# Where the recurrent gates' split input is computed: GpSimd and VectorE behind the scan, or VectorE alone ahead of it

## The chip, the cores and the metric

One core of a Trainium2 chip runs one layer of a hybrid decoder (1024 prompt rows and 8 x 4 sample rows). The metric is the device time of one execution in microseconds; the median of several runs counts.

## The reference, cut to what matters

One layer: an input projection of 1024 to 4864 columns, sliding-window attention, a gated linear recurrence (RG-LRU) with a short convolution ahead of it, gated mixing, an MLP of 4096 and a small embedding gate. All inputs are float32. The part that the change touches:

```python
def rglru(x, h0, wa, ba, wx, bx, lam):
    xb = x.reshape(B, T, RNN_BLOCKS, RNN_BS)
    r = sigmoid(einsum('btnd,nde->btne', xb, wa) + ba)
    i = sigmoid(einsum('btnd,nde->btne', xb, wx) + bx)
    log_a = -RG_C * softplus(-lam) * r
    a = exp(log_a)
    bterm = sqrt(-expm1(2.0 * log_a)) * (i * x)
    bterm = bterm.at[:, 0].add(a[:, 0] * h0)
    h = scan of h_t = a_t * h_{t-1} + bterm_t
...
xc, new_conv = causal_conv(xr, conv_prev, conv_w, conv_b)
h, h_last = rglru(xc, h0, rg_wa, rg_ba, rg_wx, rg_bx, rg_lambda)
rnn = (h * gelu(gr)) @ w_o_rnn
```

## The kernel before, in words

Activations lie transposed: 128 channels on the partitions, T = 1056 columns (1024 prompt, 32 sample) along a row, cut into three chunks of CW = 352. A float32 product is made of three matmuls on rounded parts: an operand is cast to a rounded high part (ScalarE), and its low part, operand minus high part, is a subtraction (VectorE or GpSimd). A chunk of a 1024-row projection is 24 matmuls of 352 columns (lines 228 to 230: high times high, high times low, low weight times high).

Weights arrive one 1024x128 block at a time in `wraw` (two buffers). `weights()` at the head of each `linear` splits the block that comes next, one ahead: ScalarE (or GpSimd) casts `wh` (L152), VectorE subtracts `wl` (L153), and then the next load is issued on SyncE. The recurrence's own weights (`rg`, two 128x128 pairs) are cast by ScalarE (L198) and their low part is taken by GpSimd (L199).

The order of the work is written by hand: each engine does its instructions in the order of the program. `flow` is a list of steps that are due after so many chunks; `flow.step()` after each chunk runs those that are due. A generator handed to `flow.run` goes on at each `yield n` n chunks later.

`recur(j)` runs for j = 0 to 7, one tile of 128 channels each; a tile is
- XR: projection of xr, three chunks, copied out by ScalarE (L807, L809, L810); the convolution is one ScalarE instruction (L817, with L818 for the samples) and six on VectorE (L820, L821), giving `xc`;
- the scan of the tile before, `scan()`: ScalarE's Sqrt (L865), on VectorE the product with `it` (L866), the samples' first terms (L870, L871, L872) and the scan itself (L873); after its `yield` GpSimd writes the states and multiplies with the gelu branch (L875 to L877);
- GR: projection, three chunks, gelu on ScalarE (L887). In it `gates()` runs: after the first chunk it makes `xhl`, the two tiles that hold the high part of one block of 64 channels on 64 partitions and its low part on the other 64 (L832, L833), the low part of block 0 on GpSimd and that of block 1 on VectorE, and lets GpSimd end the scan before; after the second chunk the weights of the next XR are split (L152, L153); after the third the gate matmuls of chunks 0 and 1 run (L847, L848), and their sigmoids (L849, L850) write `rt` and `it`;
- the next tile's XR: behind its first chunk the gate matmuls and sigmoids of chunk 2, then exp, exp, tanh (L855 to L857), GpSimd's `it` times `xc` (L858) and, one chunk later, VectorE's L860.

`rt`, `it`, `a` and `xhl` have one buffer each, so a tile's `rt` is free for the next tile's sigmoids only when the scan, which reads it, has ended. The gate matmuls' results lie in four banks, two per chunk.

Of the kernel before, what the change touches and what calls it, by code (L numbers as in the profile page):

```python
# [14 lines left out]
F32R = mybir.dt.float32r  # L15
AF = mybir.ActivationFunctionType
ALU = mybir.AluOpType

P = 128
# [5 lines left out]
T = NP + NS  # L25
CW = T // 3
# [64 lines left out]
def trunk(ctx: ExitStack, tc: tile.TileContext, I, O):  # L91
    nc = tc.nc
    PE, ACT, DVE, POOL, SP = nc.tensor, nc.scalar, nc.vector, nc.gpsimd, nc.sync

    def f32(ap):
        return ap.bitcast(F32)
# [27 lines left out]
    def bank():  # L124
        return po.tile([P, 512], F32, tag="o", name="o")
# [13 lines left out]
    def divide():  # L139
        if raws:  # L140
            raw, split = raws.popleft()
            ready.append(split(raw))
            fetch()
# [96 lines left out]
    def linear(xk, nk, epilogue):  # L240
        w = weights()
        for c in range(3):
            piece(w, xk, nk, c, epilogue)
            flow.step()
# [82 lines left out]
    def col(name, j, n=1):  # L327
        return vec[:, vec_at[name] + j:vec_at[name] + j + n]
# [65 lines left out]
    def halves(g):  # L394

        return slice(g * HD, (g + 1) * HD), slice((1 - g) * HD, (2 - g) * HD)
# [403 lines left out]
    def recur(j):  # L800
        xr = big.tile([P, T], F32, tag="d6", name="xr")
        xsp = const1.tile([P, NB, 7], F32, tag="xsp", name="xsp", bufs=2)
        POOL.memset(xr[:, 0:3], 0.0)

        def put_xr(c, t0, n, ps):
            if c < 2:
                ACT.copy(xr[:, 3 + t0:3 + t0 + n], ps)  # L807
            else:
                ACT.copy(xr[:, 3 + t0:3 + NP], ps[:, :n - NS])  # L809
                ACT.copy(xsp[:, :, 3:], ps[:, n - NS:].rearrange("p (s t) -> p s t", t=NT))  # L810

        POOL.tensor_copy(xsp[:, :, 0:3], state[:, j, :24].rearrange("p (s w) -> p s w", w=3))
        linear(xnk, KT, put_xr)
        xc = big.tile([P, T], F32, tag="d0", name="xc")
        xcs = xc[:, NP:].rearrange("p (s t) -> p s t", t=NT)
        cw = lambda i: col("cw", i * KT + j)
        ACT.activation(xc[:, :NP], xr[:, 3:3 + NP], AF.Identity, scale=cw(3), bias=col("cb", j))  # L817
        ACT.activation(xcs, xsp[:, :, 3:7], AF.Identity, scale=cw(3), bias=col("cb", j))  # L818
        for i in range(3):
            DVE.scalar_tensor_tensor(xc[:, :NP], xr[:, i:i + NP], cw(i), xc[:, :NP], op0=ALU.mult, op1=ALU.add)  # L820
            DVE.scalar_tensor_tensor(xcs, xsp[:, :, i:i + NT], cw(i), xcs, op0=ALU.mult, op1=ALU.add)  # L821
        POOL.tensor_copy(state[:, j, 32:35], xr[:, NP:NP + 3])
        POOL.tensor_copy(state[:, j, 0:24].rearrange("p (s w) -> p s w", w=3), xsp[:, :, 4:7])
        gl = big.tile([P, T], F32, tag=f"e{j}", name="gl")

        def gates():
            xhl = [big.tile([P, T], F32R, tag=f"d{1 + 2 * b}", name="xhl") for b in range(2)]
            for b, low in enumerate((POOL, DVE)):  # L830
                o, other = halves(b)
                ACT.copy(xhl[b][o], xc[o])  # L832
                low.tensor_tensor(xhl[b][other], xc[o], f32(xhl[b][o]), op=ALU.subtract)  # L833
            for _ in before or ():
                pass
            yield 1
            divide()
            yield 1
            wh, wl = ready.popleft()
            rt = big.tile([P, T], F32, tag="d2", name="rt")  # L840
            it = big.tile([P, T], F32, tag="d4", name="it")
            for c, (t0, n) in enumerate(CH):
                t = slice(t0, t0 + n)
                for b in range(2):
                    o, other = halves(b)
                    ps = bank()[:, :n]
                    PE.matmul(ps, wh[:, b, :], xhl[b][:, t], start=True, stop=False)  # L847
                    PE.matmul(ps, wl[:, b, :], xhl[b][:, t], start=False, stop=True)  # L848
                    ACT.activation(rt[o, t], ps[o], AF.Sigmoid, bias=col("ba", j)[o])  # L849
                    ACT.activation(it[o, t], ps[other], AF.Sigmoid, bias=col("bx", j)[o])  # L850
                if c == 1:
                    yield 1
            a = big.tile([P, T], F32, tag="d7", name="a")
            a2 = big.tile([P, T], F32, tag="d1", name="a2")
            ACT.activation(a2, rt, AF.Exp, scale=nc16[:, j:j + 1])  # L855
            ACT.activation(a, rt, AF.Exp, scale=nc8[:, j:j + 1])
            ACT.activation(rt, rt, AF.Tanh, scale=pc8[:, j:j + 1])  # L857
            POOL.tensor_tensor(it, it, xc, op=ALU.mult)  # L858
            yield 1
            DVE.scalar_tensor_tensor(rt, a2, 1.0, rt, op0=ALU.add, op1=ALU.mult)  # L860
            scans.append((a, rt, it))

        def scan():
            a, th, it = scans.popleft()
            ACT.activation(th, th, AF.Sqrt)  # L865
            DVE.tensor_tensor(th, th, it, op=ALU.mult)  # L866
            a0 = a[:, NP:].rearrange("p (s t) -> p s t", t=NT)[:, :, 0]
            b0 = th[:, NP:].rearrange("p (s t) -> p s t", t=NT)[:, :, 0]
            ah = const1.tile([P, NB], F32, tag="ah", name="ah")
            DVE.tensor_tensor(ah, a0, state[:, j, 24:32], op=ALU.mult)  # L870
            DVE.tensor_tensor(b0, b0, ah, op=ALU.add)  # L871
            DVE.memset(a0, 0.0)  # L872
            DVE.tensor_tensor_scan(a, a, th, 0.0, op0=ALU.mult, op1=ALU.add)  # L873
            yield
            POOL.tensor_copy(state[:, j, 35:36], a[:, NP - 1:NP])  # L875
            POOL.tensor_copy(state[:, j, 24:32], a[:, NP:].rearrange("p (s t) -> p s t", t=NT)[:, :, NT - 1])
            POOL.tensor_tensor(gl, a, gl, op=ALU.mult)  # L877
            rnn.append(gl)

        before = None  # L880
        if j:
            before = scan_of.popleft()()
            next(before)
        scan_of.append(scan)
        flow.run(gates(), 1)
        linear(xnk, KT,
               lambda c, t0, n, ps: ACT.activation(gl[:, t0:t0 + n], ps, AF.Gelu_apprx_tanh))  # L887

    for j in range(KT):
        recur(j)  # L890
# [418 lines left out]
    for j in range(KT):  # L1309
        j2, h2 = ((2, 1), (3, 1), (0, 1), (1, 1))[j % 4]  # L1310
        e = hidden_rows(j2, h2, F32, "e")
        for h in range(2):
            for c in range(2):
                o = slice(HALF[h].start + c * CQ, HALF[h].start + (c + 1) * CQ)
# [164 lines left out]
```

## Time and profile before

| | us |
|---|---|
| runs of the kernel, median of 3 | 1657.32 (1652.21 to 1663.13) |
| the profiled execution, its own time | 1662.28 |
| its span, first to last instruction | 1660.5 |

The profile is of one execution. Times in rows are in us from the start of the span, durations of single instructions in us or, in the grouped view, in ns. In a timeline row stand start, duration, engine, line, operation, output and inputs, shape and count, and in brackets how long the engine had been idle and what released it. PE is TensorE's matmuls, PEld its weight loads, DVE VectorE, ACT ScalarE, POOL GpSimd, SPq SyncE's queue. A duration contains some overlap with the next instruction on the engine.

### The profile page before, as it was taken

Reading aid. Unit: us, or ns where it says so; the run is one execution under the profiler, and the core shown is the slowest. Engines: PE = TensorE matmul, PEld = TensorE weight load, DVE = VectorE, ACT = ScalarE, POOL = GpSimd, SP = SyncE. Lnnn points to the kernel's source line nnn. Section 1 sums busy time; section 2 is a strip of 40 time slices with the busy share of each in tenths; the row PEclk is TensorE's granted clock in tenths of the full one; section 3 lists DMA queues with packets and bytes.
Section 4 is the critical chain, followed back from the end, with each engine's and each line's share of the span. In section 5 each row is a group of like instructions: output and inputs, shape, how many; then the busy total and the mean of one; then the engine's idle time right before and its main releaser. Section 6 shows DMA issues by size and latency. Waiting matters only on the chain.

```text
span 1660.5 us, 27447 instructions
## 1 busy us (share of the span) xinstructions
PE 1583.9 (95%) x11294; PEld 1561.7 (94%) x11294; DVE 1017.7 (61%) x1352; ACT 788.7 (48%) x1271; POOL 421.3 (25%) x348
## 2 busy tenths in 40 slices
PE   6889999998989999999999999999999999998987
PEld 5889999898989999999999999999999999998987
DVE  6697565555552144322288897479747974799653
ACT  6465656888984122322254723363336323644432
POOL 4462226345441001223444310021002100223010
PEclk9999999999999999999999999999999999999989
DMA  5422112111111113243075404541563146501222
GB/s 175 63 92 68 53 68 69 42 31 49 45 53 44 33 46 99 98 126 119 28 298 206 158 29 177 216 149 29 179 218 146 37 170 226 189 1 33 84 66 81
DMA packets 143157, 169.86 MB, mean 102 GB/s; under 512 B 19476, under 2 KB 105668, under 8 KB 143016
## 3 DMA queue, kind: packets, MB, share of 16 engines
q1 hardware_dynamic: 143032, 168.11, 30.6%
q8 instruction: 89, 1.46, 0.4%
q14 instruction: 36, 0.29, 0.1%
HBM read 138.07 MB, written 31.03 MB: 102 GB/s over the span
## 4 chain that ended last, share of the span: by engine, by line
PE 77%; DVE 13%; ACT 4%; DMA 3%; issue 3%; SPq 0%; DVEq 0%; ACTq 0%
PE m L228 12%; PE m L230 12%; PE m L229 12%; PE acc L1346 11%; PE acc L1347 10%; PE acc L1345 10%; DMA rev<-by_dist 2%; DVE ring L1143 2%; PE acc L1425 1%; PE acc L1424 1%; PE acc L1426 1%; DVE wul L1113 1%; DVE X L1187 1%; PE m L643 1%; PE o L631 1%
## 5 line engine op out<-in xcount | busy, mean ns | idle before, releaser
L1345 PE MATMUL acc<-ring,wuh 128*128 128x264 f32 x1792 | 510.2, 285 | 8.0 <-DVE X L1187 7.4
L1346 PE MATMUL acc<-ring,wuh 128*128 128x264 f32 x1792 | 513.0, 286 | 3.6 <-DVE ring L1143 3.5
L1347 PE MATMUL acc<-ring,wul 128*128 128x264 f32 x1792 | 512.2, 286 | 0.0
L1345 PEld LDWEIGHTS acc<-ring,wuh 128*128 128x128 f32 x1792 | 339.2, 189 | 8.9 <-issue 3.2
L1346 PEld LDWEIGHTS acc<-ring,wuh 128*128 128x128 f32 x1792 | 338.1, 189 | 5.3 <-DVE ring L1143 5.3
L1347 PEld LDWEIGHTS acc<-ring,wul 128*128 128x128 f32 x1792 | 338.6, 189 | 0.0
L228 PE MATMUL m<-xa,wh 128*128 128x352 f32 x912 | 299.6, 328 | 0.0
L229 PE MATMUL m<-xb,wh 128*128 128x352 f32 x912 | 297.0, 326 | 1.0 <-DVE xb L322 1.0
L230 PE MATMUL m<-xa,wl 128*128 128x352 f32 x912 | 296.8, 325 | 0.0
L229 PEld LDWEIGHTS m<-xb,wh 128*128 128x128 f32 x912 | 174.9, 192 | 2.3 <-DVE xb L322 2.0
L228 PEld LDWEIGHTS m<-xa,wh 128*128 128x128 f32 x912 | 174.7, 192 | 0.6 <-ACT xa L321 0.2
L230 PEld LDWEIGHTS m<-xa,wl 128*128 128x128 f32 x912 | 174.7, 192 | 0.0
L1108 ACT CAST wuh<-wblock 128x1024 fp32r<-128x1024 f32 x80 | 83.7, 1046 | 169.1 <-PE acc L1346 145.1
L153 DVE TENSOR_TENSOR wl<-wraw,wh 128x1024 fp32r<-128x1024 f32 (+1 forms) x61 | 71.4, 1171 | 120.6 <-ACT wh L152 102.6
L1187 DVE TENSOR_TENSOR hid<-hid,acc 128x528 f32<-128x528 f32 x112 | 76.9, 700 | 78.4 <-PE acc L1347 51.5
L1096 POOL TENSOR_TENSOR wblock<-wblock 128x1024 f32<-128x1024 f32 x10 | 27.6, 2784 | 378.2 <-DMA wblock<-in_w_down 369.9
L1187 DVE TENSOR_TENSOR X<-X,acc 128x528 f32<-128x528 f32 x156 | 104.7, 697 | 21.4 <-PE acc L1347 21.4
L1113 DVE TENSOR_TENSOR wul<-wblock,wuh 128x1024 fp32r<-128x1024 f32 x80 | 103.1, 1289 | 19.3 <-ACT wuh L1108 19.3
L1143 DVE TENSOR_TENSOR ring<-hid,ring 128x1056 fp32r<-128x1056 f32 x56 | 88.2, 1575 | 21.8 <-ACT ring L1142 21.8
L1142 ACT CAST ring<-hid 128x1056 fp32r<-128x1056 f32 x56 | 59.2, 1071 | 58.3 <-DVE hid L1126 27.5
L1424 PE MATMUL acc<-x2h,gw 128*128 128x264 f32 x256 | 76.7, 299 | 2.2 <-ACT x2h L1174 1.7
L1425 PE MATMUL acc<-x2l,gw 128*128 128x264 f32 x256 | 74.8, 292 | 2.1 <-DVE x2l L1175 2.1
(342 smaller groups left out, 3055.3 us busy)
## 6 DMA issues: line engine op xcount, KB each, us to landing
ring<-xc_dram SPq DMA_DIRECT2D x84, 528.0 KB
wraw<-in_w_in SPq DMA_DIRECT2D x34, 512.0 KB
wblock<-in_w_up SPq DMA_DIRECT2D x32, 512.0 KB
wblock<-in_w_down SPq DMA_DIRECT2D x32, 512.0 KB
xc_dram<-ring SPq DMA_DIRECT2D x28, 528.0 KB
s_dram<-sgr SPq DMA_DIRECT2D x8, 528.0 KB
sin<-s_dram SPq DMA_DIRECT2D x8, 528.0 KB
e_dram<-e SPq DMA_DIRECT2D x8, 528.0 KB
```

The costliest lines, as they stand in the source:

```text
L228: PE.matmul(ps, wh, xh, start=k == 0, stop=False)
L229: PE.matmul(ps, wh, xl, start=False, stop=False)
L230: PE.matmul(ps, wl, xh, start=False, stop=k == nk - 1)
L1108: ACT.copy(units[u][0], w_view(ph_, PRODUCTS[q][0], p2))
L1113: DVE.tensor_tensor(lo, w_view(ph_, PRODUCTS[q][0], p2), f32(hi), op=ALU.subtract)
L1143: DVE.tensor_tensor(r[:, :, 1, :], src, f32(r[:, :, 0, :]), op=ALU.subtract)
L1187: put = lambda to, of, op: DVE.tensor_tensor(to, of, ps, op=op)
L1345: PE.matmul(ps, wh[:, k, m], r[:, 0, :], start=k == 0, stop=False)
L1346: PE.matmul(ps, wh[:, k, m], r[:, 1, :], start=False, stop=False)
L1347: PE.matmul(ps, wl[:, k, m], r[:, 0, :], start=False, stop=k == 3)
L1424: PE.matmul(ps, wh, xh, start=k == 0, stop=False)
L1425: PE.matmul(ps, wh, xl, start=False, stop=False)
```

## The change

The casts and low parts of `xhl` leave `gates()` and stand in `recur` itself, behind the convolution, ahead of GR's projection. All low parts are VectorE's, in two pieces along the columns: 0 to 704 of both blocks, then 704 to 1056 of both. `scan()` gets a `yield` behind its Sqrt, so that the Sqrt stays ahead of the casts on ScalarE while the rest of the scan of the tile in front comes behind the low parts on VectorE.

```diff
         def gates():
-            xhl = [big.tile([P, T], F32R, tag=f"d{1 + 2 * b}", name="xhl") for b in range(2)]
-            for b, low in enumerate((POOL, DVE)):
-                o, other = halves(b)
-                ACT.copy(xhl[b][o], xc[o])
-                low.tensor_tensor(xhl[b][other], xc[o], f32(xhl[b][o]), op=ALU.subtract)
             for _ in before or ():
                 pass
             yield 1
...
         def scan():
             a, th, it = scans.popleft()
             ACT.activation(th, th, AF.Sqrt)
+            yield
             DVE.tensor_tensor(th, th, it, op=ALU.mult)
...
         before = None
         if j:
             before = scan_of.popleft()()
+            next(before)
+        xhl = [big.tile([P, T], F32R, tag=f"d{1 + 2 * b}", name="xhl") for b in range(2)]
+        for b in range(2):
+            o, other = halves(b)
+            ACT.copy(xhl[b][o], xc[o])
+        for t in (slice(0, 2 * CW), slice(2 * CW, T)):
+            for b in range(2):
+                o, other = halves(b)
+                DVE.tensor_tensor(xhl[b][other, t], xc[o, t], f32(xhl[b][o, t]), op=ALU.subtract)
+        if j:
             next(before)
         scan_of.append(scan)
         flow.run(gates(), 1)
```

On VectorE, in a tile of the recurrence, from the last convolution step to the low weights of the next XR; the kernel before (`rt` with `it` is the scan's product, L153 the low weights):

```order
L820 SCALAR_TENSOR_TENSOR xc<-xr,vec,xc 128x1024
L821 SCALAR_TENSOR_TENSOR xc<-xsp,vec,xc 128x32
L866 TENSOR_TENSOR rt<-rt,it 128x1056
L870 TENSOR_TENSOR ah<-a,state 128x8
L871 TENSOR_TENSOR rt<-rt,ah 128x8
L872 MEMSET a 128x8
L873 SCALAR_TENSOR_TENSOR a<-a,rt 128x1056
L833 TENSOR_TENSOR xhl<-xc,xhl 64x1056
L153 TENSOR_TENSOR wl<-wraw,wh 128x1024 x2
```

and the changed one at the same place (line numbers behind the edit differ: L862 is the product, L869 the scan):

```order
L820 SCALAR_TENSOR_TENSOR xc<-xr,vec,xc 128x1024
L821 SCALAR_TENSOR_TENSOR xc<-xsp,vec,xc 128x32
L887 TENSOR_TENSOR xhl<-xc,xhl 64x704 x2
L887 TENSOR_TENSOR xhl<-xc,xhl 64x352 x2
L862 TENSOR_TENSOR rt<-rt,it 128x1056
L866 TENSOR_TENSOR ah<-a,state 128x8
L867 TENSOR_TENSOR rt<-rt,ah 128x8
L868 MEMSET a 128x8
L869 SCALAR_TENSOR_TENSOR a<-a,rt 128x1056
L153 TENSOR_TENSOR wl<-wraw,wh 128x1024 x2
```

The low part has gone from behind the scan to ahead of its product, as four pieces in place of one; the low weights stand behind the scan in both.

On ScalarE, in a tile, from the Sqrt to the first sigmoid; the kernel before:

```order
L865 ACTIVATE rt<-rt 128x1056
L198 CAST rg<-wraw 128x256
L887 ACT_TABLE_LOAD
L887 ACTIVATE gl<-m 128x352
L832 CAST xhl<-xc 64x1056 x2
L887 ACTIVATE gl<-m 128x352
L152 CAST wh<-wraw 128x1024
L887 ACTIVATE gl<-m 128x352
L849 ACT_TABLE_LOAD
L849 ACTIVATE rt<-o,vec 64x352
```

and the changed one (L893 is the gelu, L844 the first sigmoid):

```order
L860 ACTIVATE rt<-rt 128x1056
L883 CAST xhl<-xc 64x1056 x2
L198 CAST rg<-wraw 128x256
L893 ACT_TABLE_LOAD
L893 ACTIVATE gl<-m 128x352 x2
L152 CAST wh<-wraw 128x1024
L893 ACTIVATE gl<-m 128x352
L844 ACT_TABLE_LOAD
L844 ACTIVATE rt<-o,vec 64x352
```

The two casts stand ahead of the cast of `rg` and of the gelu of the first chunk; the rest keeps its order.

## Rows read from the trace of the kernel before

**Rows 1.** The page, part 1: busy us, share of the span, instructions

```profile
PE 1583.9 (95%) x11294; PEld 1561.7 (94%) x11294; DVE 1017.7 (61%) x1352; ACT 788.7 (48%) x1271; POOL 421.3 (25%) x348
```

**Rows 2.** Waits, 345 to 490 us: who for whom, us in all, times, longest

```profile
PE o L847 <- DVE xhl L833: 13.2, 6, 2.2
...
ACT L849 <- DVE a L873: 4.5, 6, 0.8
```

**Rows 3.** Timeline of TensorE around one wait

```profile
431.68 0.32 PE L848 MATMUL o<-xhl,rg 128*128 128x352 f32 x1
434.21 0.43 PE L847 MATMUL o<-xhl,rg 128*128 128x352 f32 x1 [2.20 <-DVE xhl L833]
...
435.59 0.32 PE L230 MATMUL m<-xa,wl 128*128 128x352 f32 x1
```

**Rows 4.** Timeline of VectorE, the same tile

```profile
424.62 0.24 DVE L821 SCALAR_TENSOR_TENSOR xc<-xsp,vec,xc 128x32 f32<-128x32 f32 x1
...
425.98 0.72 DVE L821 SCALAR_TENSOR_TENSOR xc<-xsp,vec,xc 128x32 f32<-128x32 f32 x1
426.63 1.25 DVE L866 TENSOR_TENSOR rt<-rt,it 128x1056 f32<-128x1056 f32 x1
...
427.99 2.48 DVE L871 TENSOR_TENSOR rt<-rt,ah 128x8 f32<-128x8 f32 x1
...
430.51 2.36 DVE L873 TENSOR_TENSOR_SCAN a<-a,rt 128x1056 f32<-128x1056 f32 x1
432.90 1.25 DVE L833 TENSOR_TENSOR xhl<-xc,xhl 64x1056 fp32r<-64x1056 f32 x1
434.19 1.23 DVE L153 TENSOR_TENSOR wl<-wraw,wh 128x1024 fp32r<-128x1024 f32 x1
```

**Rows 5.** Timeline of GpSimd, the same tile

```profile
425.11 1.55 POOL L199 TENSOR_TENSOR rg<-wraw,rg 128x256 fp32r<-128x256 f32 x1 [3.98 <-ACT rg L198]
427.96 2.47 POOL L833 TENSOR_TENSOR xhl<-xc,xhl 64x1056 fp32r<-64x1056 f32 x1 [1.30 <-ACT xhl L832]
...
437.86 1.04 POOL L152 CAST wh<-wraw 128x1024 fp32r<-128x1024 f32 x1
```

**Rows 6.** Windows, one tile: length; busy of PE, PEld, DVE, ACT, POOL; clock, DMA

```profile
404.40:431.74 27.34, 25.14 (x158) 24.84 (x156) 15.71 (x16) 23.93 (x34) 12.78 (x11) 1.00 0.16 44
```

**Rows 7.** Timeline of ScalarE, from one tile's first sigmoid to the next one's

```profile
406.90 0.55 ACT L849 ACTIVATE rt<-o,vec 64x352 f32<-64x352 f32 x1
...
412.08 0.46 ACT L807 COPY xr<-m 128x352 f32<-128x352 f32 x1 [0.66 <-PE m L230]
...
420.27 0.43 ACT L809 COPY xr<-m 128x320 f32<-128x320 f32 x1 [0.34 <-PE m L230]
...
420.78 1.24 ACT L817 ACTIVATE xc<-xr,vec 128x1024 f32<-128x1024 f32 x1
...
423.64 1.09 ACT L865 ACTIVATE rt<-rt 128x1056 f32<-128x1056 f32 x1
...
426.74 2.17 ACT L832 CAST xhl<-xc 64x1056 fp32r<-64x1056 f32 x2
...
432.95 1.28 ACT L849 ACT_TABLE_LOAD   x1 [0.76 <-DVE a L873]
```

**Rows 8.** Groups of VectorE by shape: busy us, mean ns; idle before

```profile
L955 DVE TENSOR_TENSOR ml<-sin,mh 128x352 fp32r<-128x352 f32 x24 | 12.6, 526 | 38.4 <-ACT mh L954 38.4
...
L153 DVE TENSOR_TENSOR wl<-wraw,wh 128x512 fp32r<-128x512 f32 x8 | 5.5, 687 | 20.5 <-ACT wh L152 20.5
```

**Rows 9.** Waits of SyncE's queue, 395 to 460 us

```profile
SPq L162 <- POOL rg L199: 39.9, 3, 13.3
```

**Rows 10.** Timeline of ScalarE, the first tile

```profile
283.35 1.07 ACT L703 COPY kt<-o 128x512 f32<-128x512 f32 x2
```

**Rows 11.** Windows behind two of the waits, columns as in rows 6

```profile
323.00:327.00 4.00, 4.00 (x17) 4.00 (x16) 3.41 (x9) 3.89 (x7) 1.58 (x4) 0.57 0.11 25
...
490.00:494.00 4.00, 4.00 (x17) 4.00 (x17) 0.12 (x1) 3.88 (x8) 2.44 (x1) 0.57 0.46 135
```

## The prediction, made before the changed kernel ran

> **What bounds the kernel now.** I read the page first: TensorE is busy 95% of the span, so a change elsewhere counts only where TensorE waits [rows 1]. Then the list of waits over the stretch of the recurrence that has no attention work left in it (345 to 490 us), because the change touches only this stage. TensorE waits there in one place, six times in six tiles: the first gate matmul that reads the second xhl tile (L847) waits 2.2 us for VectorE's low part L833; ScalarE's sigmoids L849 wait six times for VectorE's scan L873 [rows 2]. Next I read one steady tile engine by engine. I call s the start of its ACT xc (L817), 420.78 us.
>
> TensorE: the gate matmuls of block 0 run at 431.68 and those of block 1 only at 434.21; at full pace they would come 0.16 later, so 2.4 us are lost per tile [rows 3]. VectorE shows why: the conv ends, then come rt*it (L866), a tiny sum L871 that takes 2.48 us for 8 elements, the scan L873, and only then the low part L833, at 432.90 = s+12.1 [rows 4]. L871 is long because GpSimd's low part of block 0 runs from 427.96 to 430.43 and L871 ends when it does [rows 4, 5]. One tile takes 27.34 us, of which TensorE is busy 25.14 and ScalarE 23.93 [rows 6]. So TensorE could save 2.2 us per tile, but ScalarE has only 3.4 us to spare, and this is what decides. Its order from the first sigmoid of a tile to the next xc is 406.90 to 420.78, 13.88 us, with two short waits for TensorE in it, 0.66 and 0.34 [rows 7]: 12.8 us when nothing makes it wait (1.0 off for the waits, 0.1 for the overlap of neighbours).
>
> **The change, part by part.** It removes GpSimd's 2.47 us per tile [rows 5] and VectorE's one 1.25 us [rows 4]; it adds four VectorE pieces, 64x704 twice and 64x352 twice, and puts ScalarE's two casts ahead of the GR part and the pieces ahead of the scan. I follow the tile again from s.
> - Conv: the last L821 ended late at 426.70 only because GpSimd's rg low part L199 ran beside it (1.55 us) [rows 4, 5]. L199 needs ScalarE's rg cast, which now stands behind the two xhl casts, so L199 moves away; alone the last L821 takes 0.24, as the one before it does, and ends at 426.22 = s+5.45.
> - ScalarE: its Sqrt ends at 424.73 = s+3.95 [rows 7]. It used to go on with rg and gelu; now the cast stands next and waits for the conv, 1.5 us idle that were not there. Casts take 2.17 [rows 7]: s+5.5 to s+7.7.
> - Pieces: no row has 64x704. By rows it lies between a 128x512 of 0.69 and the 64x1056 of 1.25 [rows 4, 8]; by its length between the two, 0.89, of which 0.81 until the next can start. A 352-column one takes 0.53 [rows 8], 0.45 until the next. The first piece runs beside the second cast; the second starts at s+7.7, and then the two short ones: s+9.4 without disturbance. The rg cast ends at s+8.1, so L199 (0.7 alone: 1.55 less the 0.87 that it waited until 425.98) falls among them; they end at s+9.9. I take this collision as certain, since L199 and L821 show it in this profile [rows 4, 5].
> - Scan group: L866 to L873 starts, with L871 short since GpSimd has nothing left to run there (its next step waits for the scan), takes 1.6 until the scan begins (1.36 from the start of L866 to that of L871, and an estimated 0.25 for L871 and the memset behind it, as little as operations on 8 elements allow) and the scan 2.36 [rows 4]. It ends at s+13.9, where it ended at 432.87 = s+12.1 before.
> - What is late next: sigmoids. They write rt, which the scan still reads; table load and sigmoids follow the scan end within 0.1 us [rows 2, 7]. Scan end s+13.95, table load 1.28, first sigmoid s+15.3, plus 12.8 without waits: the next xc at s+28.1, against 27.34 before.
> - TensorE: the pieces for the first two chunks are there at s+8.6, and it comes to them at about s+12, so the old wait is gone. But the next projection's low weights (L153) stand on VectorE behind the scan, as before: scan end s+13.9, plus 1.23 [rows 4]: the first matmul on them (L230) starts at s+15.2. From there TensorE has 22 matmuls, 4 gate matmuls, 5 chunks of 24 and 8 gate matmuls, all in all 156 x 0.159 = 24.9 us, so 3.2 of the 28.1 are waiting: the wait moves from L847 to L230 and grows from 2.4 to 3.2. Its XR chunks end at s+27.1, 0.4 before ScalarE comes to copy the last of them, so TensorE no longer sets the length of the tile.
> - SyncE: the weight load freed by L199 [rows 9] is issued 3.4 us later; its reader, GpSimd's cast L152, starts at 437.86, 11 us after L199 ended [rows 5], and load and cast keep room. I cost it at nothing; if the room were used up, it would be up to 3.4 us per tile.
>
> Sum against the profiled execution: six intervals between tiles at +0.75, 4.5 us. The first tile: its kt copies (L703) followed the casts at 283.35 [rows 10] and now come behind rg, table load and two gelus as well; I take 1.1 of that as seen in the end, since ScalarE works there without a pause. The last tile: its successor's L230 0.5 later. Clock: TensorE ran at its lower level (granted 0.57 of full in a 4 us window, mostly 1.2 GHz) after three of the seven waits, of which the first and the last stand in [rows 11]; 17 matmuls took 4.0 us where 17 x 0.159 (25.14 over 158, rows 6) is 2.7, so 1.3 each. After longer waits I expect one or two more, +2. Together +8: 1662.28 + 8 for an execution like the profiled one, which lay 5 above the median of the runs shown, so 1657.3 + 8 = 1665.
>
> Bounds: without the L199 collision 27.4 per tile, +0.4 in six; with each 352 piece as long as the 0.69 of a 128x512 and 704 as long as 1.25, 28.8, +9. First and last tile 0 to 3. Clock from none low (-4) to all seven (+5). The own range is 1654 to 1673.
>
> [...]
>
> **Rivals.**
> 1. The wait simply goes. TensorE then needs 25.1 per tile: 7 x 2.4 = 16.8 and the three slow stretches, 4, are saved: 1637. For it: L833 is the only wait of TensorE in this stage [rows 2]. Against: it needs the sigmoids not to follow the scan, and the scan not to be later; both stand in the rows.
> 2. The collision does not happen, or the pieces are quicker: 27.4 per tile, +0.4 and the rest: 1661. For it: L199's start hangs on a cast that could slip past the pieces. Against: the cast ends in the middle of them.
> 3. Slower: the wait at L230 drops TensorE's clock after every tile and for twice as long as now, so that XR's first chunk runs wholly at 1.2 GHz: 7 x 2.6 - 4 = 14, with the 6 of the rest +20: 1677. It decides from the point where TensorE, late by more than ScalarE's 0.4 us lead at the next XR copy, sets the tile instead. For it: rows 11, and the longer wait. Against: none of the low stretches in this profile outlasted 4 us.
> 4. The change does not give what it says: the first gate matmul waits for the short pieces too. They end at s+9.9, before TensorE comes: nothing changes against the forecast.
>
> **How the numbers follow.** Forecast (with 4) 0.66, rival 2 0.17, rival 1 0.08, rival 3 0.09. The likeliest gives 1665. The range leaves out rival 1 and the far part of 3: 1651 to 1675, the lower end also since the three runs shown lie 5 us to either side of their median. 1%, 16.6 us, is about what a measurement of this kernel can tell from no change: faster by more than that is rival 1 alone, 0.08, slower the upper part of rival 3 and a tail of the bounds, 0.08, the rest within.
>
> **What would show it.** In the changed kernel's waits TensorE no longer waits at the gate matmul for xhl but for VectorE's wl (L153) at L230, some 3 us per tile; the scan ends near s+14; the small sum L867 takes under 0.3 us; ScalarE idles 1.5 us before its first xhl cast and some 2 us before the sigmoid table load; L199 takes over 1 us amid the pieces; tiles are 28 us apart. Wrong would be: tiles 26 us apart or less, sigmoids that start before the scan ends, or a wait on a weight load.

## The result, and the profile after

| | before | after |
|---|---|---|
| median of 6 runs each, us | 1658.78 (1652.21 to 1663.15) | 1670.69 (1663.9 to 1674.76) |
| ratio after to before | | 1.0071, 95% interval 1.0048 to 1.0094 |
| profiled execution, us | 1662.28 | 1663.90 |

The changed kernel is slower by 0.7%, 11.9 us between the medians, within the 1% that the prediction calls no change. The two profiled executions lie only 1.6 us apart: that of before, 1662.28, is near the upper end of the six runs beside it, and that of after is the fastest of its six. So the comparison below goes by tiles, and a second profile of each kernel stands at the end of the experiments.

The page of the changed kernel, part 1:

```profile
PE 1580.7 (95%) x11294; PEld 1558.6 (94%) x11294; DVE 1011.9 (61%) x1376; ACT 787.1 (47%) x1271; POOL 390.7 (24%) x340
```

Against [rows 1] GpSimd has lost 30.6 us: its eight low parts, 8 x 2.47 = 19.8 [rows 5], and time in which instructions of both engines had stretched each other (L199, for one, takes 1.01 in place of the 1.55 of [rows 5]). VectorE has 24 instructions more, three in each tile, and is busy 5.8 us less. No engine is busier, and the kernel is slower: the answer lies in the waits. These are the changed kernel's over the recurrence, 270 to 525 us (columns as in [rows 2]):

```profile
PE m L230 <- DVE wl L153: 17.2, 6, 3.0
ACT L844 <- DVE a L869: 15.7, 6, 2.6
ACT xhl L883 <- DVE xc L821: 14.6, 8, 3.9
```

TensorE's wait for the low part of `xhl` (L847 in [rows 2]) is gone. In its place TensorE waits six times for the low weights of the next XR, up to 3.0 us. ScalarE's wait for the scan ahead of the sigmoids has grown from 0.8 to 2.6, and a wait for the convolution, ahead of the casts, comes in all eight tiles. One tile, s = 424.00, on VectorE, answering to [rows 4]:

```profile
429.19 0.25 DVE L821 SCALAR_TENSOR_TENSOR xc<-xsp,vec,xc 128x32 f32<-128x32 f32 x1
430.59 0.88 DVE L887 TENSOR_TENSOR xhl<-xc,xhl 64x704 fp32r<-64x704 f32 x1 [1.14 <-ACT xhl L883]
431.69 2.40 DVE L887 TENSOR_TENSOR xhl<-xc,xhl 64x704 fp32r<-64x704 f32 x3 [0.21 <-ACT xhl L883]
434.10 1.26 DVE L862 TENSOR_TENSOR rt<-rt,it 128x1056 f32<-128x1056 f32 x1
435.28 0.16 DVE L866 TENSOR_TENSOR ah<-a,state 128x8 f32<-128x8 f32 x1
435.47 0.17 DVE L867 TENSOR_TENSOR rt<-rt,ah 128x8 f32<-128x8 f32 x1
435.60 0.07 DVE L868 MEMSET a<- 128x8 f32 x1
435.70 2.36 DVE L869 TENSOR_TENSOR_SCAN a<-a,rt 128x1056 f32<-128x1056 f32 x1
437.97 1.20 DVE L153 TENSOR_TENSOR wl<-wraw,wh 128x1024 fp32r<-128x1024 f32 x1
```

GpSimd, ScalarE and TensorE of the same tile, answering to [rows 5], [rows 7] and [rows 3]:

```profile
432.16 1.01 POOL L199 TENSOR_TENSOR rg<-wraw,rg 128x256 fp32r<-128x256 f32 x1 [7.44 <-ACT rg L198]
...
438.12 1.10 POOL L871 COPY state<-a 128x1 f32<-128x1 f32 x1 [4.95 <-DVE a L869]
```

```profile
424.00 1.24 ACT L817 ACTIVATE xc<-xr,vec 128x1024 f32<-128x1024 f32 x1
...
429.48 2.17 ACT L883 CAST xhl<-xc 64x1056 fp32r<-64x1056 f32 x2 [1.53 <-DVE xc L821]
...
438.13 1.28 ACT L844 ACT_TABLE_LOAD   x1 [2.62 <-DVE a L869]
439.43 0.55 ACT L844 ACTIVATE rt<-o,vec 64x352 f32<-64x352 f32 x1
...
444.70 0.46 ACT L807 COPY xr<-m 128x352 f32<-128x352 f32 x1 [0.76 <-PE m L230]
...
452.98 0.43 ACT L809 COPY xr<-m 128x320 f32<-128x320 f32 x1 [0.43 <-PE m L230]
```

```profile
439.23 0.43 PE L230 MATMUL m<-xa,wl 128*128 128x352 f32 x1 [3.05 <-DVE wl L153]
```

The tiny sum (L867) takes 0.17 us in place of L871's 2.48 [rows 4], as GpSimd has nothing beside it. But the pieces stand ahead of it, and the scan ends at 438.06 = s+14.06. Within 0.1 us of that ScalarE starts its table load, and the low weights start on VectorE behind the scan; TensorE's L230 follows them. Two windows, one per tile, columns as in [rows 6], and behind them, within the second, the 4 us that follow the wait at L230:

```profile
395.77:424.00 28.23, 25.52 (x160) 25.23 (x159) 14.37 (x19) 23.68 (x33) 8.67 (x11) 1.00 0.15 43
424.00:453.49 29.49, 26.44 (x156) 26.15 (x155) 15.42 (x19) 23.77 (x33) 9.02 (x11) 0.94 0.14 41
...
440.00:444.00 4.00, 4.00 (x17) 4.00 (x17) 1.05 (x1) 3.84 (x7) 2.92 (x4) 0.57 0.15 33
```

A tile at full clock takes 28.23 us where it took 27.34 [rows 6]; one in which the granted clock falls behind the wait (0.57 of full in those 4 us, as in [rows 11]) takes 29.49. In that tile ScalarE waits for TensorE at two XR copies, 0.76 and 0.43 us, which is the 1.2 that it is longer; in the other it has no such wait. So TensorE sets the tile with the slow stretch, and ScalarE the other. The lower level, which the prediction writes as 1.2 GHz, shows in the trace as a granted clock of 0.50 (441 to 443 us) and one 352-column matmul every 0.293 us, 1.2 columns per ns (nine of them from 441.01 to 443.65); behind it, at a granted 1.00, one comes every 0.16 us.

### The profile page after: what moved, and what is told of

Same layout as the page of the kernel before. It is cut to its first block, busy times and chain, and to the rows that moved or that the text cites. A ratio compares the mean times of both kernels' runs of the same rounds, so it can differ in the third digit from the quotient of the medians.

```text
span 1662.2 us, 27447 instructions
## 1 busy us (share of the span) xinstructions
PE 1580.7 (95%) x11294; PEld 1558.6 (94%) x11294; DVE 1011.9 (61%) x1376; ACT 787.1 (47%) x1271; POOL 390.7 (24%) x340
## 4 chain that ended last, share of the span: by engine, by line
PE 66%; DVE 15%; ACT 7%; DMA 6%; issue 4%; SPq 0%; POOL 0%; DVEq 0%; ACTq 0%
PE m L228 10%; PE m L230 10%; PE m L229 10%; PE acc L1352 9%; PE acc L1351 9%; PE acc L1353 9%; DVE ring L1149 2%; DMA rev<-by_dist 2%; DVE wul L1119 2%; PE acc L1431 1%; PE acc L1430 1%; PE acc L1432 1%; DVE xc L820 1%; DMA wraw<-in_w_in 1%; DVE X L1193 1%
## 5 line engine op out<-in xcount | busy, mean ns | idle before, releaser
L230 PE MATMUL m<-xa,wl 128*128 128x352 f32 x912 | 298.2, 327 | 17.2 <-DVE wl L153 17.2
L230 PEld LDWEIGHTS m<-xa,wl 128*128 128x128 f32 x912 | 175.0, 192 | 19.0 <-DVE wl L153 19.0
L153 DVE TENSOR_TENSOR wl<-wraw,wh 128x1024 fp32r<-128x1024 f32 (+1 forms) x61 | 71.3, 1169 | 124.3 <-ACT wh L152 105.2
```

The lines of the kernel that those rows point to most:

```text
L230: PE.matmul(ps, wl, xh, start=False, stop=k == nk - 1)
```

## The experiments

A tile's length is the distance between two starts of ACT xc (L817). "Steady" are the tiles from the third on, which have no attention work left beside them; "clean" is one in which the granted clock stays at 1.00, and "low" one in which it falls for a stretch.

**The same four pieces, behind the scan.** If the order on VectorE is what costs, the cut into pieces on VectorE alone must gain when it stands behind the scan, as before. The edit is made in the kernel before.

```diff
-            for b, low in enumerate((POOL, DVE)):
+            for b in range(2):
                 o, other = halves(b)
                 ACT.copy(xhl[b][o], xc[o])
-                low.tensor_tensor(xhl[b][other], xc[o], f32(xhl[b][o]), op=ALU.subtract)
+            for t in (slice(0, 2 * CW), slice(2 * CW, T)):
+                for b in range(2):
+                    o, other = halves(b)
+                    DVE.tensor_tensor(xhl[b][other, t], xc[o, t], f32(xhl[b][o, t]), op=ALU.subtract)
```

> Half of the change: all low parts on VectorE in two pieces, but left where they were, behind the scan. Theory (GpSimd's low part held the scan up, and the sigmoids follow the scan): the small sum L874 takes under 0.3 us, the scan ends near s+9.9 instead of s+12.1, the pieces near s+12.4, the next low weights near s+13.6 instead of s+14.6; steady tiles 26.0 us apart against 27.34 before, TensorE's wait per tile 1.1 us, no low clock behind it, the whole 9 to 14 us shorter than before. Rival (moving GpSimd's half to VectorE only lengthens the queue that TensorE waits for): tiles 27.3 to 28.6, no gain.

Measured: 1687.65 us (4 runs) against 1660.09 of the kernel before (7 runs), ratio 1.0157 (1.013 to 1.0185): slower than both kernels. VectorE, GpSimd and TensorE of one tile, s = 404.87:

```profile
412.31 2.36 DVE L876 TENSOR_TENSOR_SCAN a<-a,rt 128x1056 f32<-128x1056 f32 x1
414.70 5.90 DVE L836 TENSOR_TENSOR xhl<-xc,xhl 64x704 fp32r<-64x704 f32 x4
420.64 2.36 DVE L153 TENSOR_TENSOR wl<-wraw,wh 128x1024 fp32r<-128x1024 f32 x2
...
415.73 3.08 POOL L880 TENSOR_TENSOR gl<-a,gl 128x1056 f32<-128x1056 f32 x1
...
421.92 0.66 PE L230 MATMUL m<-xa,wl 128*128 128x352 f32 x1 [3.79 <-DVE wl L153]
```

The scan does end early, at s+9.8. But its end releases GpSimd's product with the gelu branch (L880), which takes 3.08 us and now falls among the pieces: the four take 5.90 us. The low weights come later than in any other kernel here, TensorE waits 3.79, and this tile is 32.44 us long (404.87 to 437.31) at a granted clock of 0.89. The expectation had overlooked who is released by the earlier scan. So this run does not decide on the order; it points to a second one, between GpSimd's product and VectorE's pieces, which a run further down tests.

**The order alone.** In the changed kernel block 0 goes back to GpSimd and both blocks are whole, but they stay ahead of the scan.

```diff
-        for b in range(2):
+        for b, low in enumerate((POOL, DVE)):
             o, other = halves(b)
             ACT.copy(xhl[b][o], xc[o])
-        for t in (slice(0, 2 * CW), slice(2 * CW, T)):
-            for b in range(2):
...
+            low.tensor_tensor(xhl[b][other], xc[o], f32(xhl[b][o]), op=ALU.subtract)
```

> The other half alone: casts and low parts ahead of the scan, but block 0 on GpSimd and both whole, as before. Theory (what is ahead of the scan delays it by its own length, and GpSimd's 2.47 us now stand in the way of VectorE's low part): scan ends near s+15, steady tiles 29 us apart, slower than the changed kernel by 0.7 to 0.9 a tile. Rival (the four pieces on VectorE are what costs): tiles below 28.2, near 27.3.

Measured: 1671.29 us, one execution; the one clean tile is 28.86 us, 1.5 more than before:

```profile
398.19:427.05 28.86, 25.64 (x160) 25.21 (x159) 14.14 (x16) 23.68 (x34) 11.76 (x12) 1.00 0.15 42
```

So the place ahead of the scan costs even without the pieces. In the changed kernel, VectorE's taking both blocks, in pieces, is a gain of 0.6 per tile over this (0.7 to 0.9 had been expected), not the loss.

**A second buffer for `rt`, in the changed kernel.** If the sigmoids set the tile by waiting for the scan that reads `rt`, another buffer sets them free, and the tile falls only to what TensorE's wait for the low weights allows.

```diff
-            rt = big.tile([P, T], F32, tag="d2", name="rt")
+            rt = big.tile([P, T], F32, tag=f"e{j + 2}" if 1 <= j <= 5 else "d2", name="rt")
```

> The changed kernel with other buffers for rt in tiles 1 to 5, so that the sigmoids need not wait for the scan. Theory (the sigmoids behind the scan set the tile, and TensorE's wait for the low weights behind the scan stands 0.4 to 0.6 us below that): the sigmoids' table load starts near s+11.8 with no wait for the scan, tiles 27.5 to 27.8 us apart instead of 28.23, TensorE still waits 2.5 us or so at L230. Rival A (the low weights alone set the tile): 28.2 unchanged. Rival B (the sigmoids alone): 25.6 to 26.

Measured: 1675.99 us, one execution. ScalarE's table load and VectorE's scan in a clean tile (s = 339.97), and the windows of that tile and of the longest:

```profile
351.50 1.28 ACT L844 ACT_TABLE_LOAD   x1
...
351.66 2.36 DVE L869 TENSOR_TENSOR_SCAN a<-a,rt 128x1056 f32<-128x1056 f32 x1
```

```profile
339.97:367.83 27.86, 25.15 (x158) 24.86 (x157) 14.82 (x19) 23.78 (x34) 8.65 (x11) 1.00 0.15 43
428.02:458.73 30.71, 28.00 (x158) 27.71 (x157) 14.89 (x19) 23.77 (x34) 8.62 (x11) 0.89 0.14 39
```

The sigmoids no longer wait, their table load starts before the scan, and the clean tile goes from 28.23 to 27.86 (27.5 to 27.8 had been expected). The two waits therefore lie close behind each other: with the sigmoids free, TensorE's 25.15 of work and its wait of 2.7 at L230 make up the whole 27.86. The kernel as a whole is no faster: four steady tiles are 29.5 to 30.7 long. TensorE now sets the tile, so that a stretch at the lower clock counts in full. And three of the four tiles are 30.64 to 30.71, and by that their stretches last longer: a mean granted clock of 0.89 over 30.71 us is some 7 us at the lower level of 0.50 (an estimate, 0.11 x 30.71 / 0.50), where the 0.94 over the changed kernel's tile above is some 4 (440 to 444). Why they last longer is not shown.

**The same buffer in the kernel before**, where the sigmoids' wait should set the tile little.

```diff
-            rt = big.tile([P, T], F32, tag="d2", name="rt")
+            rt = big.tile([P, T], F32, tag=f"e{j + 2}" if 1 <= j <= 5 else "d2", name="rt")
```

> The kernel before with other buffers for rt in tiles 1 to 5. Theory (before, TensorE's wait for the low part behind the scan set the tile, and the sigmoids' wait did not): steady tiles 27.3 us apart, unchanged. Rival (the sigmoids' wait set it before, too): 26.5 or less.

ScalarE's table load, which waits for nothing, and TensorE's first gate matmul on the second `xhl` tile:

```profile
404.15 1.28 ACT L849 ACT_TABLE_LOAD   x1
...
406.13 0.43 PE L847 MATMUL o<-xhl,rg 128*128 128x352 f32 x1 [2.18 <-DVE xhl L833]
```

Measured: 1659.9 us, one execution, and a tile of 27.37 (392.70 to 420.07), as before. TensorE's 2.18 at L847 is what sets the tile before the change.

**The pieces behind the scan, with GpSimd held back.** This tests the reading of the first experiment. The pieces stay behind the scan, the end of the scan's generator is called behind the low weights, and a copy of one element onto itself on VectorE, which GpSimd's first copy then has to wait for, keeps GpSimd's product behind the low weights. The diff is against the kernel of the first experiment.

```diff
-            for _ in before or ():
-                pass
             yield 1
             divide()
+            for _ in before or ():
+                pass
...
             DVE.tensor_tensor_scan(a, a, th, 0.0, op0=ALU.mult, op1=ALU.add)
             yield
+            DVE.tensor_copy(a[:, NP - 1:NP], a[:, NP - 1:NP])
             POOL.tensor_copy(state[:, j, 35:36], a[:, NP - 1:NP])
```

> The low parts on VectorE behind the scan as in the first run, but GpSimd's end of the scan (states, product with the gelu branch, 2.5 us) held back until the next low weights are made, by a one-column copy of the scan's result onto itself behind them on VectorE. Theory (in the first run that product stood between the pieces: 5.9 us for four pieces that take 2.6 alone): scan ends near s+9.9, the four pieces take 2.6 us, low weights end near s+13.6; steady tiles 25.9 to 26.2 us apart, TensorE waits about 1.1 us per tile and its clock stays up; 8 to 14 us faster than the kernel before. Rival (pieces on VectorE behind the scan are slow in themselves): tiles above 28 as in the first run.

Measured: 1652.35 us (9 runs) against 1659.27 of the kernel before (13 runs), ratio 0.9958 (0.994 to 0.9975). One tile, s = 388.49:

```profile
398.30 2.91 DVE L836 TENSOR_TENSOR xhl<-xc,xhl 64x704 fp32r<-64x704 f32 x4
401.24 1.23 DVE L153 TENSOR_TENSOR wl<-wraw,wh 128x1024 fp32r<-128x1024 f32 x1
...
402.87 2.48 POOL L881 TENSOR_TENSOR gl<-a,gl 128x1056 f32<-128x1056 f32 x1
...
402.52 0.43 PE L230 MATMUL m<-xa,wl 128*128 128x352 f32 x1 [0.81 <-DVE a L878]
```

```profile
388.49:415.23 26.74, 25.59 (x158) 24.88 (x157) 15.03 (x20) 23.93 (x34) 8.30 (x11) 1.00 0.16 45
```

The four pieces take 2.91 (2.6 had been expected) in place of 5.90: the difference, 2.99, is about the product's 3.08. The product itself, alone, takes 2.48. This shows that the product was what slowed the pieces in the first experiment, and that the pieces on VectorE alone gain when nothing stands in their way. The trace puts the wait of 0.81 down to the added copy (L878), but that copy follows L153, which ends at 402.47: L230 at 402.52 waited for the low weights. The tile is 26.74 us, 0.5 over the expectation's upper end. That is not the waits: the 0.81 and 0.33 at the gate matmuls (L850) make up the 1.1 that was expected. TensorE is busy 25.59 in place of 25.14 [rows 6], and why is not shown. The granted clock is 1.00 in this tile, and the five steady ones are 26.72 to 26.74 long, so it stays up in them.

**Long pieces, low weights, short pieces.** The order that follows from it: only the long pieces are wanted by the first gate matmuls, so the low weights can go ahead of the short ones. The diff is against the kernel of the experiment above.

```diff
-            for t in (slice(0, 2 * CW), slice(2 * CW, T)):
-                for b in range(2):
...
+            def lows(t):
+                for b in range(2):
...
+            lows(slice(0, 2 * CW))
             yield 1
             divide()
+            lows(slice(2 * CW, T))
             for _ in before or ():
                 pass
```

> The same, with the next tile's low weights between the long and the short pieces. Theory: low weights end near s+12.8, TensorE's wait per tile falls to 0.8 us or less, tiles 25.6 to 25.9 us apart, now set by ScalarE, which has no room left; 10 to 16 us faster than before. Rival (ScalarE sets the tile at 26 anyway): no difference to the run without this step.

Measured: 1647.7 us (5 runs), ratio 0.9927 (0.9896 to 0.9958): 11.6 us faster than the kernel before and faster than the changed one by more.

```profile
388.54:414.13 25.59, 25.26 (x158) 24.83 (x157) 15.03 (x20) 23.91 (x34) 8.50 (x11) 1.00 0.17 47
```

```profile
398.36 1.80 DVE L836 TENSOR_TENSOR xhl<-xc,xhl 64x704 fp32r<-64x704 f32 x2
400.19 1.23 DVE L153 TENSOR_TENSOR wl<-wraw,wh 128x1024 fp32r<-128x1024 f32 x1
401.45 1.07 DVE L836 TENSOR_TENSOR xhl<-xc,xhl 64x352 fp32r<-64x352 f32 x2
...
400.22 0.43 PE L853 MATMUL o<-xhl,rg 128*128 128x352 f32 x1 [0.33 <-DVE xhl L836]
```

TensorE is busy 25.26 of the tile's 25.59 us and waits 0.33 in it. The tile is now TensorE's own work, as rival 1 of the prediction had it (25.1), and not set by ScalarE, as the expectation had it. This is what VectorE's taking both low parts can give in another order, with GpSimd's product held back.

**`rg`'s low part on VectorE, behind the scan, in the changed kernel.** Without L199 on GpSimd the pieces meet nothing.

```diff
-            POOL.tensor_tensor(rg[:, 2:4, :], wr, f32(rg[:, 0:2, :]), op=ALU.subtract)
+            DVE.tensor_tensor(rg[:, 2:4, :], wr, f32(rg[:, 0:2, :]), op=ALU.subtract)
```

> The changed kernel with the low part of rg on VectorE, behind the scan, so that GpSimd has nothing to do beside the pieces. Theory (the collision with GpSimd costs 0.6 us of the scan's end and of the tile, one for one): the three later pieces take 1.8 instead of 2.40, the scan ends near s+13.45 instead of s+14.06, clean tiles 27.6 to 27.8 us apart instead of 28.23. Rival (the collision is hidden): 28.2 to 28.6.

```profile
406.67 1.96 DVE L887 TENSOR_TENSOR xhl<-xc,xhl 64x704 fp32r<-64x704 f32 x3 [0.21 <-ACT xhl L883]
...
412.51 0.40 DVE L199 TENSOR_TENSOR rg<-wraw,rg 128x256 fp32r<-128x256 f32 x1
...
412.96 0.66 PE L843 MATMUL o<-xhl,rg 128*128 128x352 f32 x1 [2.90 <-DVE rg L199]
```

Measured: 1673.49 us, one execution. The three later pieces take 1.96 in place of 2.40, and the scan ends at s+13.59 (s = 399.00) in place of s+14.06: the collision costs 0.4 to 0.5 of the scan's end. On the tile it is inconclusive: 28.10 (429.76 to 457.85), between the two expectations' ranges, because the edit made a wait of its own. `rg`'s low part is behind the scan now, and TensorE waits 2.90 for it at the first gate matmul.

**The changed kernel without the cut.** Both low parts are whole and on VectorE, ahead of the scan.

```diff
-        for t in (slice(0, 2 * CW), slice(2 * CW, T)):
+        for t in (slice(0, T),):
```

> The changed kernel without the cut: one 64x1056 low part per block. Theory (each piece more costs its fixed part, and TensorE is not waiting for the first pieces): the scan ends 0.1 to 0.2 us earlier, clean tiles 28.0 to 28.15 us apart. Rival (the cut is what lets TensorE start early): TensorE waits at the gate matmuls again and tiles grow by 0.5 or more.

Measured: 1661.07 us, one execution, and a clean tile of 27.73 (422.50 to 450.23), 0.3 to 0.4 below what was expected.

```profile
400.20 2.54 DVE L887 TENSOR_TENSOR xhl<-xc,xhl 64x1056 fp32r<-64x1056 f32 x2 [1.14 <-ACT xhl L883]
402.77 1.69 DVE L862 TENSOR_TENSOR rt<-rt,it 128x1056 f32<-128x1056 f32 x1
...
404.79 2.36 DVE L869 TENSOR_TENSOR_SCAN a<-a,rt 128x1056 f32<-128x1056 f32 x1
...
401.77 1.57 POOL L199 TENSOR_TENSOR rg<-wraw,rg 128x256 fp32r<-128x256 f32 x1 [7.43 <-ACT rg L198]
```

From the start of the first low part to that of the scan are 4.59 us here and 5.11 in the changed kernel (430.59 to 435.70). The two whole low parts take 2.54; the four pieces take 0.88 and 2.40 with a gap between them, since the short first piece is done before the second cast is. L199 does not escape here: it meets the product L862, which takes 1.69 in place of 1.26, so its collision costs 0.4 with and without the cut, and the 0.5 between the two runs is the cut's own. (With the cut and no collision, in the run with `rg` on VectorE, the same stretch takes 4.65.) In this place nothing reads the early columns any sooner: TensorE waits for the scan's followers. The whole execution, 1661.07, lies within the runs of the kernel before (1653.9 to 1664.86).

**Both kernels profiled again**, for the part that differs from execution to execution, the clock.

> The changed kernel once more, for a second profile. Open is why its runs are 12 us longer while the first profile shows 7 to 8 in this stage. Theory (its longer wait lets TensorE's clock fall behind more tiles than the first profile happened to show): clean tiles 28.2, low-clock tiles 29.5 us apart, at least four of the seven low, the stage 9 to 11 us longer than in the first profile of the kernel before. Rival (the rest lies outside the stage): two or three low tiles here, and lower clock in other stages.

> The kernel before once more, for a second profile to set beside it. Theory: clean tiles 27.34 us apart, low-clock ones 28.8, two or three of the seven low. Rival (its first profile was an unlucky one): none or one low.

Measured: 1668.9 us for the changed kernel and 1656.58 for the one before, one execution each. Two tiles of the changed kernel and two of the one before:

```profile
337.99:367.44 29.45, 26.55 (x157) 26.26 (x156) 15.40 (x19) 23.75 (x33) 9.01 (x11) 0.94 0.15 41
...
455.48:483.71 28.23, 25.52 (x160) 25.23 (x159) 14.37 (x19) 23.68 (x33) 8.67 (x11) 1.00 0.16 43
```

```profile
304.74:335.46 30.72, 27.31 (x162) 26.20 (x161) 20.34 (x30) 25.23 (x41) 13.14 (x12) 0.94 0.14 39
...
417.60:445.00 27.40, 25.21 (x158) 24.93 (x157) 15.71 (x16) 23.93 (x35) 12.76 (x12) 1.00 0.16 44
```

Of the seven tiles from the first xc to the eighth, the granted clock falls in five in the changed kernel (three in its first profile) and in one in the kernel before (two in its first). So the changed kernel did as expected (the stage is 8.9 us longer than in the first profile before), and for the kernel before the rival held, with one low tile. That agrees with the longer wait letting the clock fall more often. The mean granted clocks of whole executions agree too: 0.979 to 0.986 in the changed kernel's six, the median 0.981, and 0.983 to 0.990 in the twenty of the kernel before that stand beside the experiments, the median 0.987. How often the clock falls behind a wait is known only roughly, from two profiles each.

## Why the prediction was right

**The likeliest case came true in its mechanism:** 1670.7 us where 1665 was forecast, inside 1651 to 1675, with a change below 1% and the old wait replaced by a longer one. The number alone would not tell: it lies 5.7 above the forecast and 6.3 below the 1677 of rival 3. The tiles tell, step by step:

- Conv, casts, pieces: conv at s+5.44 (5.45 was predicted), ScalarE idle 1.53 ahead of the first cast (1.5), pieces of 0.88 and later (0.89), their end s+10.1 (9.9). The collision with L199 was there: 1.01 us on GpSimd amid pieces, and worth 0.4 to 0.5 by the `rg` experiment.
- VectorE and GpSimd slowed each other where their instructions ran side by side. Three measurements show it: the pieces at 2.40 with L199 and 1.96 without, at 5.90 with the product and 2.91 without, and GpSimd's one-column copy, 1.10 us beside VectorE's L153 (L871) and 0.19 behind it in the run with GpSimd held back.
- The tiny sum: 0.17 (under 0.3). Scan end s+14.06 (13.9). Sigmoids follow it, idle 2.62 (some 2). The second buffer for `rt` showed that they set the clean tile and that TensorE's L230 stands 0.4 behind.
- TensorE: L847's wait gone, L230's 2.71 and 3.05 in neighbouring tiles (3.2). Against the kernel before that is no gain, and this is why a 95% busy TensorE did not speed up. The prediction's list of matmuls between two waits (22, 4, 5 x 24 and 8) adds up to 154; the 156 that it uses is right, with the two that run ahead of the next L230, and 156 x 0.159 is 24.8. The forecast does not hang on it.
- The weight load behind L199, put at nothing: GpSimd's L152 waited for it once, 3.3 us in the first tile, and TensorE had no wait for low weights there.
- The collision-free rival 2 and the full gain of rival 1 did not come. Rival 3, slower since TensorE sets the tile at the lower clock, came in part: TensorE does set the low tiles (29.49 against 28.24). But the clock fell behind some waits only, and of the eight low stretches in the seven tiles of both profiles one lasted about 7 us (321 to 328 in the first, a granted 0.50 up to 327 and a mean of 0.89 over its tile), the others some 4 (means of 0.94 and 0.95), where rival 3 has the long stretch in every tile.

**The sizes were low.** Means of the two profiles of each kernel, first xc to eighth: 199.5 us before (200.19, 198.85), 208.6 after (208.15, 209.11), +9.1. Of it, the first tile is 0.97 (32.16 against 31.19; 1.1 was predicted). Six tiles at +0.87 (28.23 against 27.37) are 5.2, where 0.75 and 4.5 were predicted: the scan ended 0.15 later than summed. What is left, 2.9, agrees with the clock: four low tiles against one and a half, each 1.2 longer (29.49 less 28.24); predicted were one or two more, 2. Up to the last A copy ahead of the next stage the difference is 9.6, inside the interval of the ratio (8.0 to 15.6 us). These four executions as wholes differ by only 7.0 (1666.4 against 1659.4): outside this stretch the changed kernel's two are 2.6 shorter, for which the change gives no reason. So the 11.9 between the medians is not accounted for in full. The median of the changed kernel's six granted clocks is 0.981, and its two profiled executions have 0.986 and 0.985, so more low tiles in the other runs would fit; no profile shows them.

**The price of the cut was in the sum, but not seen.** The sum has the pieces' durations nearly right; it never sets them against whole low parts, and the expectation of the run without the cut put the difference at 0.1 to 0.2 per tile. It is 0.5. From run to run (one execution each, the clean tiles) it goes from 27.37 before to 28.86 with casts and low parts ahead of the scan (+1.5), to 27.73 with both low parts on VectorE (-1.1), and to 28.23 with the cut (+0.5). So the place costs most, the engine wins most of that back, and without the cut the change would have lost 0.36 per tile in place of 0.87.

## What to carry to other kernels

A wait is worth its length only if what the change puts later on the same engine has nobody waiting. Here the scan and the low weights stood behind the moved work on VectorE, and sigmoids and TensorE behind those; read down the engine's order to the next item that another engine wants, and put the work behind that (long pieces, low weights, short pieces: 0.9927 of the time before). When VectorE finishes something earlier, look at what it releases on GpSimd, since the two slowed each other here (four pieces at 5.90 in place of 2.91 us, the product at 3.08 in place of 2.48); a one-element copy on VectorE can hold GpSimd back until the urgent work is done (1652 in place of 1688 us). Cut an operation only where the first piece has a reader that would otherwise wait.

## What was not expected of the hardware

- How dear a wrong order between VectorE and GpSimd is: four short VectorE instructions at 5.90 in place of 2.91 us, for one GpSimd product of 2.48 us.
- A wait of some 3 us on TensorE costs more than itself: the clock falls behind many of them, here to 0.57 of full in a 4 us window, and a tile that holds such a stretch is 1.2 us longer in the changed kernel. With the second `rt` buffer, where TensorE sets the clean tile too, one such tile was 1.6 longer (29.49 against 27.86) and one with some 7 us at the lower level, by its mean granted clock of 0.89, 2.85 (30.71). Behind waits of the same kernel it fell sometimes and sometimes not, in three of seven tiles in one execution and in five of seven in the next; at 1.2 us each, two more low tiles are 2.4 us between executions.
